# First pair of a GEGLU MLP kernel: the late pieces of x through one PSUM bank, and four products moved ahead of them

## The chip, the cores and the metric

The kernel runs on one core of one Trainium2 chip. The metric is the time of one execution in device microseconds (us). Smaller is better.

PE is the engine of matrix products and transposes, PEld its weight loads, DVE and ACT the two elementwise engines used here, POOL the fourth, SP the engine that issues most DMAs (transfers from the large memory). PE writes into PSUM, a memory of eight banks; the other operands lie in SBUF.

## The reference

```python
# x: 8 x 1024 x 1024, w_gate and w_up: 1024 x 4096, w_down: 4096 x 1024, float32
gate = x @ w_gate
up = x @ w_up
gate = 0.5 * gate * (1 + np.tanh(np.sqrt(2 / np.pi) * (gate + 0.044715 * gate ** 3)))
return ((gate * up) @ w_down).astype(np.float32)
```

## The kernel before

It works in eight passes of 1024 tokens and takes the columns of the two first weights in pairs of 128-column blocks. Nearly all products use a scheme that needs sums of blocks of x and of the weights. The very first pair cannot: its data are still landing. It has its own routine, which casts pieces of x to half precision on DVE, transposes them on PE into a PSUM bank, copies the bank to SBUF, and computes plain products into the eight PSUM banks. K is the dimension that a product sums over; it is taken in two halves (kh). A bank is named by token half (mh), column block (j) and weight (w):

```python
bank = {(mh, j, w): 4 * mh + 2 * j + w ...}          # (1,0,1) is bank 5, (1,1,1) is bank 7

def product(mh, kh, w, j, c=full):                    # 4 matmuls; kh: half of K; c: half or all of the 512 tokens
    for k in range(KH):
        nc.tensor.matmul(ps_all[:, bank[mh, j, w], c], raw(0, 0)[:, w, kh * KH + k, j * P : (j + 1) * P],
                         xq[f"b{kh + 1}{mh + 1}"][:, k, c], start=(kh == 0 and k == 0 and c.start == 0), ...)

def x0_transpose(mh, gp, kh, b, copy):                # 8 transposes into bank b, one copy out of it
    ...
    copy(o, ps)
```

The end of the routine prepares the second pair: a last weight cast, then the four sums of x blocks (`sum_x`, 1.2 us each) and the weight sums (`sum_w`), all on DVE:

```python
    cast_first(0, 1, c1)
    cast_first(1, 1, c1, dve)
    ...                                               # the banks are given back
    sum_x(1); sum_w(0, 1, 0); sum_w(0, 1, 1); sum_x(2)
    outputs(1, 0); outputs(1, 1)
    sum_x(3); sum_w(0, 1, 2); sum_w(0, 1, 3); sum_x(4)
```

## Time and profile before

| what | value |
|---|---|
| time, median of the first 3 runs | 2256.03 us |
| span of the profiled run | 2253.6 us |
| PE busy | 2245.6 us |
| PE waits listed, whole execution | 3.75 us in five places |
| second pair starts on PE (called S) | 27.31 us |
| products on x behind the sums (called M) | 38.16 us |

The timeline of PE in the kernel before (start us, us, engine, line, operation; in brackets the idle time before it and what ended it):

```profile
27.31 3.62 PE L635 MATMUL ps<-x_b,ring 128*128 128x512 f16 x16
30.77 3.73 PE L635 MATMUL ps<-x_sums,ring 128*128 128x512 f16 x16
34.68 3.64 PE L635 MATMUL ps<-x_sums,ring 128*128 128x512 f16 x16 [0.19 <-DVE ring L360]
38.16 3.62 PE L635 MATMUL ps<-x_b,ring 128*128 128x512 f16 x16
```

The second line starts at 30.77 and the third at 34.68, 3.91 us for 16 products that need 3.45. The bracket admits only 0.19, because it counts from the modelled end of the last product (0.38 us each, overlapping; 0.35 between the starts) and because a short stop inside the second group (3.73 against 3.62 us, 0.11) is not broken out.

### The profile page before, as it was taken

The page shows a single profiled execution, that of the slowest core. Times are in us where ns is not written, and L with a number is a line of the kernel's source. Part 1 is how long each engine was busy: PE and PEld are TensorE (multiplying, and loading weights), DVE is VectorE, ACT ScalarE, POOL GpSimd, SP SyncE. Part 2 cuts the span into 40 slices and gives each one's busy share as a digit, 9 for nine tenths or more (in the row PEclk, how much of TensorE's full clock was granted, in tenths as well). Part 3 has the DMA queues.
Part 4 walks back from the last instruction along what each step waited for, and adds up shares of the span by engine and source line. Part 5 has one row for each costly group of instructions (what it writes and reads, how often), then busy time and mean ns, then how long its engine had stood idle before and what let it go on. Part 6 is the DMA issues. An engine that isn't in the chain of part 4 may idle for free.

```text
span 2253.6 us, 42764 instructions
## 1 busy us (share of the span) xinstructions
PE 2245.6 (100%) x16616; PEld 1624.2 (72%) x16616; DVE 1565.1 (69%) x2187; ACT 955.4 (42%) x1863; POOL 674.6 (30%) x825
## 2 busy tenths in 40 slices
PE   9999999999999999999999999999999999999999
PEld 4444444444444445888888888888888888888888
DVE  6666458883588755877776677666786667866674
ACT  4443135651365622666125550356404653055520
POOL 1332013330133300555014540255403543044520
PEclk9999999999999999999999999999999999999999
DMA  9898969999999999999998999988998889998886
GB/s 243 164 210 215 289 180 243 258 270 291 243 229 249 281 304 352 332 343 366 302 337 276 320 309 310 324 267 328 314 322 314 283 310 317 322 309 276 285 292 225
DMA packets 309117, 642.46 MB, mean 285 GB/s; under 512 B 79088, under 2 KB 185328, under 8 KB 288368
## 3 DMA queue, kind: packets, MB, share of 16 engines
q1 hardware_dynamic: 254128, 566.57, 73.5%
q0 software_dynamic: 54784, 73.14, 19.5%
q8 instruction: 130, 2.13, 0.4%
q14 instruction: 75, 0.61, 0.1%
HBM read 574.36 MB, written 138.41 MB: 316 GB/s over the span
## 4 chain that ended last, share of the span: by engine, by line
PE 87%; DMA 2%; SPq 1%; DVE 0%; issue 0%; DVEq 0%
PE ps L857 40%; PE ps L1108 20%; PE ps L635 17%; PE ps L1000 10%; DMA wd_quads<-x_sums 1%; SPq L255 0%; DMA ring<-wd_ops 0%; DVE x_sums L278 0%; DVE h_a L932 0%; DVE tmp L1177 0%; SPq L496 0%; DVEq L278 0%; SPq L544 0%
## 5 line engine op out<-in xcount | busy, mean ns | idle before, releaser
L857 PEld LDWEIGHTS <-ring 128*128 128x128 f16 x8320 | 814.1, 98 | 94.4
L834 POOL TENSOR_TENSOR h_a<-tmp 128x256 f16<-128x256 f32 x640 | 468.0, 750 | 840.6 <-ACT tmp L822 833.5
L857 PE MATMUL ps<-x_sums,ring 128*128 128x256 f16 x5760 | 655.8, 273 | 0.0
L819 DVE TENSOR_TENSOR tmp<-tmp,ps 128x512 f32<-128x512 f32 x640 | 414.3, 683 | 147.1 <-PE ps L857 90.2
L635 PEld LDWEIGHTS <-ring 128*128 128x128 f16 x2632 | 257.4, 98 | 311.2 <-DVE ring L360 0.9
L804 ACT COPY tmp<-ps 128x512 f32<-128x512 f32 x520 | 304.2, 585 | 237.0 <-PE ps L857 163.3
L635 PE MATMUL ps<-x_sums,ring 128*128 128x512 f16 x1504 | 340.1, 379 | 0.2 <-DVE ring L360 0.2
L822 ACT ACTIVATE tmp<-tmp 128x256 f32<-128x256 f32 x640 | 263.7, 418 | 173.2 <-DVE tmp L817 79.5
L857 PE MATMUL ps<-x_b,ring 128*128 128x256 f16 x2560 | 305.6, 273 | 0.0
L817 DVE TENSOR_TENSOR tmp<-ps,tmp 128x512 f32<-128x512 f32 x240 | 165.4, 689 | 145.2 <-ACT tmp L804 99.8
L635 PE MATMUL ps<-x_b,ring 128*128 128x512 f16 x1128 | 259.1, 379 | 0.0
L661 POOL TENSOR_TENSOR h_a<-tmp 128x512 f16<-128x512 f32 x94 | 141.1, 1501 | 377.4 <-ACT tmp L659 265.3
L1108 PEld LDWEIGHTS <-h_a 128*128 128x128 f16 x2240 | 219.2, 98 | 25.3
L1000 PE MATMUL ps<-ring,h_a 128*128 128x512 f16 x1024 | 222.3, 379 | 0.6 <-DMA ring<-wd_ops 0.6
L1108 PE MATMUL ps<-ring,h_a 128*128 128x256 f16 x1920 | 216.1, 273 | 0.0
L1000 PEld LDWEIGHTS <-h_a 128*128 128x128 f16 x1152 | 112.6, 98 | 136.8 <-DMA ring<-wd_ops 1.1
L654 DVE TENSOR_TENSOR tmp<-ps,tmp 128x512 f32<-128x512 f32 x188 | 127.3, 685 | 108.0 <-ACT tmp L646 106.5
L1165 ACT ACTIVATE tmp<-ps 128x512 f32<-128x512 f32 x60 | 35.3, 597 | 362.6 <-PE ps L1108 274.6
L1177 DVE SCALAR_TENSOR_TENSOR tmp<-ps,tmp 128x512 f32<-128x512 f32 x120 | 81.1, 690 | 97.5 <-PE ps L1108 66.7
L360 DVE TENSOR_TENSOR ring<-ring 128x1024 f16<-128x1024 f16 x188 | 139.7, 757 | 11.7 <-DMA ring<-in_w_up_dram 7.5
L646 ACT COPY tmp<-ps 128x512 f32<-128x512 f32 x188 | 109.8, 586 | 77.8 <-PE ps L635 77.8
L1108 PE MATMUL ps<-ring,x_sums 128*128 128x256 f16 x1120 | 126.3, 273 | 0.0
(102 smaller groups left out, 1534.0 us busy)
## 6 DMA issues: line engine op xcount, KB each, us to landing
ring<-w_ops SPq DMA_DIRECT2D x480, 512.0 KB, 4.9
ring<-wd_quads SPq DMA_DIRECT2D x110, 1024.0 KB, 6.9
ring<-wd_ops SPq DMA_DIRECT2D x35, 1024.0 KB, 8.2
out_dram<-tmp SPq DMA_DIRECT2D x128, 256.0 KB, 6.6
w_ops<-h_s SPq DMA_DIRECT2D x128, 256.0 KB, 6.8
ring<-in_w_gate_dram POOLq DMA_DIRECT2D x23, 1024.0 KB, 10.6
ring<-in_w_up_dram POOLq DMA_DIRECT2D x23, 1024.0 KB, 17.9
wd_quads<-x_sums SPq DMA_DIRECT2D x131, 128.0 KB, 6.5
```

The costliest lines, as they stand in the source:

```text
L360: nc.vector.tensor_tensor(o, a, b, op)
L635: nc.tensor.matmul(ps(b, w), lhs[:, k], rhs[:, k, :], start=(first and k == 0), stop=(k == KH - 1), skip_group_check=True,)
L654: nc.vector.tensor_tensor(o, ps("b", w), o, ADD)
L661: nc.gpsimd.tensor_tensor(hq[TO[n]][:, i, :], tmp[:, t[n, 1]], tmp[:, t[n, 0]], MUL)
L804: nc.scalar.copy(tmp[:, t[o[1]]], ps_all[:, bank[o[2]]])
L817: nc.vector.tensor_tensor(d, b, a, SUB)
L819: nc.vector.tensor_tensor(d, a, b, ADD if o[4] == "add" else SUB)
L822: nc.scalar.activation(d, d, GELU, scale=GSC)
L834: nc.gpsimd.tensor_tensor(h, tmp[:, t[o[1]], MQ : 2 * MQ], g, MUL)
L857: nc.tensor.matmul(ps_all[:, bank[c], w * MQ : (w + 1) * MQ], lhs[:, w, k], rhs[:, k], start=(first and w == 0 and k == 0), stop=(k == KH ...
L1000: nc.tensor.matmul(ps_all[:, bank[b, g]], lhs[:, j, g * P : (g + 1) * P], dc[:, n, :], start=(first and j == 0), stop=(j == NP - 1), skip_ ...
L1108: nc.tensor.matmul(ps_all[:, bank[c], m * MQ : (m + 1) * MQ], lhs[:, j, m * P : (m + 1) * P], rhs[:, j, :], start=(first and j == 0 and m ...
```

## The change

The apparent intent: while the second half of x lands, PE should have work. The four products of bank 7 on the first half of K are ready early, but bank 7 was needed for transposes. So the late pieces of x all go through bank 5, bank 7's products move forward, and bank 5's products move to the end.

```diff
         for c in (lo, hi):
             for j in range(2):
                 product(1, 0, 0, j, c)
+        product(1, 0, 1, 1)
         x0_cast(0, 0, 1)
-        x0_transpose(0, 0, 1, 5, act)
         x0_cast(0, 1, 1)
-        x0_transpose(0, 1, 1, 7, dve)
+        x0_transpose(0, 0, 1, 5, dve)
         halves(1)
-        product(1, 0, 1, 0)
+        x0_transpose(0, 1, 1, 5, dve)
         cast_first(1, 1, c0, dve)
         product(0, 1, 0, 0)
         product(0, 1, 0, 1)
         x0_cast(1, 0, 1)
-        x0_transpose(1, 0, 1, 7, act)
+        x0_transpose(1, 0, 1, 5, act)
         x0_cast(1, 1, 1)
         product(0, 1, 1, 0)
         product(0, 1, 1, 1)
-        x0_transpose(1, 1, 1, 7, dve)
+        x0_transpose(1, 1, 1, 5, dve)
...
-            for w, j in ((0, 0), (0, 1), (1, 0)):
+            for w, j in ((0, 0), (0, 1), (1, 1)):
                 product(1, 1, w, j, c)
         for kh in range(2):
-            product(1, kh, 1, 1)
+            product(1, kh, 1, 0)
```

## The prediction

> **What bounds the kernel now.** I read the page first (busy times, then the chain that ended last), then the list of waits of the TensorE (PE), then the timeline of the first 31 us, because the change edits only the routine for the first pair of columns of the first pass.
>
> ```profile
> span 2253.6 us, 42764 instructions
> ...
> PE 2245.6 (100%) x16616; PEld 1624.2 (72%) x16616; DVE 1565.1 (69%) x2187; ACT 955.4 (42%) x1863; POOL 674.6 (30%) x825
> ...
> PE 87%; DMA 2%; SPq 1%; DVE 0%; issue 0%; DVEq 0%
> ```
>
> PE is busy for 2245.6 of 2253.6 us and is 87% of the last chain. Everything else counts only where it makes PE wait. The waits of PE, over the whole execution (total, times, longest):
>
> ```profile
> PE ps L1227 <- DVE h_s L1230: 1.6, 1, 1.6
> PE ps L314 <- DVE h_a L304: 0.7, 1, 0.7
> PE ps L1206 <- ACT x_b L317: 0.7, 1, 0.7
> PE ps L1000 <- DMA ring<-wd_ops: 0.6, 1, 0.6
> PE ps L635 <- DVE ring L360: 0.2, 1, 0.2
> ```
>
> Only the third lies in what is edited. No change of this kind can win more than about 0.7 us, 0.03% of the time. The fourth (at 278.93 us) and the fifth (at 34.68 us) are the two later places where a delay of PE could be taken up again. The timeline around the third (start us, us, engine, line; brackets: idle before, and what ended it):
>
> ```profile
> 14.23 1.98 PE L1206 MATMUL ps<-x_b,ring 128*128 128x256 f16 x16
> 14.44 0.69 DVE L317 COPY x_b<-ps 128x1024 f16<-128x1024 f16 x1 [1.74 <-PE ps L314]
> ...
> 15.04 1.28 DVE L304 TENSOR_SCALAR h_a<-h_a 128x1024 f16<-128x1024 f32 x2
> ...
> 16.05 1.06 PE L314 MATMUL ps<-identity,h_a 128*128 128x128 f16 x16
> ...
> 16.70 1.01 ACT L317 COPY x_b<-ps 128x1024 f16<-128x1024 f16 x1 [2.56 <-PE ps L314]
> ...
> 17.14 0.69 DVE L317 COPY x_b<-ps 128x1024 f16<-128x1024 f16 x1 [0.81 <-PE ps L314]
> ...
> 17.76 2.75 PE L1206 MATMUL ps<-x_b,ring 128*128 128x512 f16 x12 [0.65 <-ACT x_b L317]
> ...
> 19.08 0.69 DVE L304 TENSOR_SCALAR h_a<-h_a 128x1024 f16<-128x1024 f32 x1 [0.65 <-DMA h_a<-in_x_dram]
> 20.34 0.61 PE L314 MATMUL ps<-identity,h_a 128*128 128x128 f16 x8
> 20.44 0.69 DVE L304 TENSOR_SCALAR h_a<-h_a 128x1024 f16<-128x1024 f32 x1 [0.67 <-DMA h_a<-in_x_dram]
> ```
>
> The reader is to see three things. First, the two pieces of x that open the second half of K are cast from 15.04 us on (two casts, no DMA wait in front): they have landed before PE asks for them at 16.05. Second, PE then does both groups of 8 transposes in one go, into banks 5 and 7, and two engines empty the banks side by side (ACT from 16.70, DVE from 17.14). Third, the only gap is that of the next product, which writes bank 5 and therefore waits for ACT's copy to end (16.70 + 1.01 = 17.71, PE starts at 17.76). From there to 27.31 us PE has no wait: the last two pieces of x land at 19.08 and 20.44, and PE takes them only at 20.34 and 22.52.
>
> **What the Trainium skill says.** "PSUM — Partial Sum Buffer", section "PSUM bank collisions raise a hardware error": two engines must not be in one bank and quadrant at once, the hardware doesn't arbitrate, so semaphores must guard by bank. The trace agrees: the wait of 0.65 us ends 0.05 us after the copy out of bank 5. "TensorE: Matmul & The Clock Gate", Part 4 (PE-mode transpose): a transpose lands in PSUM and needs a copy after it, some 275 ns in one kernel, and doesn't count as PE-busy for the clock gate. Here one lasts 219 ns and groups issue at (16.89 - 16.05)/15 = 0.056 us. Same page, Part 1: after at least one idle window of about 3.4 us the array falls to half rate. At the start this trace shows the half rate (weight loads of the first products at 9.29, 9.72, 10.14, 0.43 us apart) and later 0.215 us (12 products in 17.76 to 20.34); it shows no fall back.
>
> **The change part by part.** Bank 7 is product (second half of tokens, w 1, j 1); bank 5 is (same half, w 1, j 0).
>
> 1. *Four matmuls of bank 7 on the first half of K move ahead of the transposes, four of bank 5 move to the end.* PE work is unchanged: 4 x 0.215 = 0.86 us each way. Bank 7 and x are ready (DVE copy ends at 14.44 + 0.69 = 15.13), so they run at 16.05 to 16.91. The old wait of 0.65 us, in issue time 17.76 - (16.05 + 16 x 0.056) = 0.81 us, is gone.
> 2. *Both groups of transposes go through bank 5.* Now transposes, copy, transposes, copy, product are one serial chain with no other PE work inside it. Group one: starts 16.91, last result 0.61 later, 17.52. DVE copies 0.04 later, 17.56, for 0.69, to 18.25. Group two may write bank 5 at 18.30: result 18.91, copy 18.95 to 19.64. The product of the first tokens on the second half of K reads both pieces: 19.70. PE's issue is empty from 16.91 + 0.45 = 17.36 to 18.30 (0.94) and from 18.75 to 19.70 (0.95): 1.89 us.
> 3. *Net on PE.* Before, that product began four matmuls after 17.76, at 18.62. After: 19.70. That is +1.08 us, equal to 1.89 - 0.81.
> 4. *Copy by DVE in place of ACT (0.69 for 1.01).* It shortens the first link by 0.32, already in the sum. DVE then does its weight cast at 19.65 to 20.33 and the next x cast to 21.0; PE asks for that piece at 19.70 + 8 x 0.215 = 21.42. No wait.
> 5. *The last two pieces also through bank 5.* Transposes at 21.42, ACT copy to about 23.04; 8 matmuls stand between, to 23.58, so bank 5 is free when the last group comes. DVE copy to about 24.95; the half-width products between (12 x 0.11 = 1.3, from 24.03) hide it. No wait.
> 6. *To the end of the pair.* From there 4.35 us of products as before (22.96 to 27.31): next pair at 28.38 instead of 27.31, +1.07.
> 7. *Behind it.* DVE's chain of sums starts at 27.40, after a wait of 2.27 us for a weight piece, so DMA and not PE sets it; its outputs end at some 26.4 instead of 25.1, still in time. So the sums come when they came, and the wait of 0.19 us at 34.68 vanishes. Left: about +0.9 us. At 278.93 PE waits 0.60 us for a load of wd_ops. The chain in front of it goes through small stores and DVE sums; DVE follows PE there without a gap from about 204 to 232 us (its step at 209.30 was released by PE), and the queue's loads wait for PE. So that wait moves with PE and takes up little. From 278.93 on PE runs without a wait: the delay reaches the end.
>
> Sum: 1.08 - 0.19 = +0.89, to which I add 0.1 for the chance of a clock fall (below): 2256.03 + 1.0 = **2257.0 us**.
>
> **The rivals.**
> *The fill pays.* If x landed late, four matmuls ready to run would be worth up to the old gap, 0.81: about 2255.2. Against it: no DMA wait stands before the casts at 15.04, so PE was not waiting for x but for the copies; the fill is spent before the gap opens. I give it 7%.
> *The delay is taken up later.* If the load at 278.93 keeps its own time, 0.60 goes: +0.3, about 2256.3. For: a chain of DMAs stands before it, and their landing varies. Against: the DVE and queue waits in front of it follow PE. 20%.
> *The clock falls.* Between 16.91 and 19.70 only transposes run: 2.79 us (before: 17.76 - 16.05 = 1.71). By the page's window of 3.4 us this is too short; if a partly idle window were enough, one window at half rate costs some 1.7 us, two 3.4: about 2259 to 2260. 8%.
> *DVE becomes the bound.* One more copy, 0.69 us, against an idle stretch of 2.27 before 27.40. It would need another 1 us of lateness; the waits at 30 to 37 us would then grow. 5%, some +1.5.
>
> **Range and chances.** The main path gives 2256.9, repeats of the kernel before spread over 0.6 us, and the take-up at 278.93 can move it by as much. The pull of the late clock case makes the upper side longer: 2255.7 to 2258.3. All cases lie inside 0.2% of the time before, so within 2% is near certain: faster 0.01, same 0.98, slower 0.01.
>
> **What would show each step right or wrong.** In the timeline of after: 4 full products directly behind the half-width ones at about 16.05; two separate groups of 8 transposes at 16.9 and 18.3 with two DVE copies between; two waits of PE on DVE's x_b copies, about 0.75 to 0.95 us each, in place of the one on ACT; the first product of the second half at 19.7; the next pair at 28.4; no PE wait near 34.7; matmuls still 0.215 us apart. Wrong would be: PE going on with other work during the copies, x landing after 16 us in that run, the next pair starting before 27.3, or the wait near 279 us shrinking by as much as PE is late.

## More of the kernel before

The granted clock is the share of its full rate that PE was given, 1.000 at most.

S and M are read from the timeline of PE. Between them lie 48 products of 512 columns, first 16 on x and then 32 on sums of x; they issue 0.2155 us apart, so M - S is 10.34 us if PE never stops. Here it is 10.85: PE stands still for about half a microsecond in all.

## The result and the profile after

| | median | range | runs |
|---|---|---|---|
| before, same rounds and the first three | 2255.91 us | 2254.71 to 2256.97 | 6 |
| after | 2255.53 us | 2255.22 to 2257.07 | 6 |

The ratio is 0.9999, with a 95% interval of 0.9986 to 1.0012: no difference that these runs could show. A ratio here is the mean time of one kernel's fast runs over the mean of the other's fast runs of the same rounds, so it is not quite the ratio of the medians above. The predicted 2257.0 was too high, and the measured median lies 0.17 us below the range.

Yet the trace after shows the local loss almost as it was worked out. The list of PE's waits in the changed kernel (total us, times, longest):

```profile
PE ps L1227 <- DVE h_s L1230: 1.6, 1, 1.6
PE ps L314 <- DVE x_b L317: 0.8, 1, 0.8
PE ps L1206 <- DVE x_b L317: 0.8, 1, 0.8
PE ps L314 <- DVE h_a L304: 0.8, 1, 0.8
PE ps L1000 <- DMA ring<-wd_ops: 0.4, 1, 0.4
```

The single wait on ACT's copy (0.7) has become two waits on DVE's copies (0.8 each), and the wait on DVE's weight sums (0.2) is gone. The timeline of the changed kernel around them:

```profile
14.15 2.84 PE L1206 MATMUL ps<-x_b,ring 128*128 128x256 f16 x20
...
16.83 0.61 PE L314 MATMUL ps<-identity,h_a 128*128 128x128 f16 x8
17.48 0.69 DVE L317 COPY x_b<-ps 128x1024 f16<-128x1024 f16 x1 [1.23 <-PE ps L314]
18.22 0.61 PE L314 MATMUL ps<-identity,h_a 128*128 128x128 f16 x8 [0.78 <-DVE x_b L317]
...
18.86 0.69 DVE L317 COPY x_b<-ps 128x1024 f16<-128x1024 f16 x1 [0.70 <-PE ps L314]
...
19.61 1.89 PE L1206 MATMUL ps<-x_b,ring 128*128 128x512 f16 x8 [0.78 <-DVE x_b L317]
...
28.30 3.62 PE L635 MATMUL ps<-x_b,ring 128*128 128x512 f16 x16
...
31.75 7.07 PE L635 MATMUL ps<-x_sums,ring 128*128 128x512 f16 x32
...
38.66 3.62 PE L635 MATMUL ps<-x_b,ring 128*128 128x512 f16 x16
```

Transposes, copy, transposes, copy, product now stand one behind the other. From the start of the half-width products to the first product on the second half of K it takes 19.61 - 14.15 = 5.46 us; before it took 18.62 - 14.23 = 4.39. That is the +1.07 of the prediction. The second pair starts 0.99 later (28.30 against 27.31). But M comes only 0.50 later (38.66 against 38.16): behind S, PE now runs 48 products without a stop. In this pair of traces, half of the loss has been given back within 10 us.

### The profile page after: what moved, and what is told of

Same layout as the page of the kernel before. It is cut to its first block, busy times and chain, and to the rows that moved or that the text cites. A ratio compares the mean times of both kernels' runs of the same rounds, so it can differ in the third digit from the quotient of the medians.

```text
span 2254.2 us, 42763 instructions
## 1 busy us (share of the span) xinstructions
PE 2245.5 (100%) x16616; PEld 1624.4 (72%) x16616; DVE 1563.9 (69%) x2188; ACT 955.6 (42%) x1862; POOL 684.5 (30%) x825
## 4 chain that ended last, share of the span: by engine, by line
PE 84%; DMA 3%; DVE 1%; SPq 1%; issue 0%; ACT 0%; POOL 0%; POOLq 0%; DVEq 0%
PE ps L857 40%; PE ps L1108 20%; PE ps L635 14%; PE ps L1000 10%; DMA ring<-in_w_up_dram 2%; DMA wd_quads<-x_sums 1%; SPq L255 0%; DMA ring<-wd_ops 0%; DVE ring L360 0%; DVE x_sums L278 0%; DVE h_a L672 0%; DVE h_s L278 0%; DVE tmp L654 0%; POOL ring L345 0%; DVE h_a L932 0%
## 5 line engine op out<-in xcount | busy, mean ns | idle before, releaser
L661 POOL TENSOR_TENSOR h_a<-tmp 128x512 f16<-128x512 f32 x94 | 149.7, 1592 | 367.8 <-ACT tmp L659 265.4
```

What stands on the lines that cost most here:

```text
L661: nc.gpsimd.tensor_tensor(hq[TO[n]][:, i, :], tmp[:, t[n, 1]], tmp[:, t[n, 0]], MUL)
```

## The experiments

All outputs are right. "Same call" means the runs of the kernel before on the same chip in the same rounds (9 each). S and M as above; the last trace column is when PE begins the products behind a load of wd_ops (prepared blocks of the third weight), with the wait listed there. From M to that point PE needs 240.0 us without a stop. In filled_sums PE's wait is listed under a step of DVE; its weight load waited 1.85 us for the load there, as in the others.

| run | S | M | M - S | behind the load (wait) | mean less mean of before, same call |
|---|---|---|---|---|---|
| before | 27.31 | 38.16 | 10.85 | 278.93 (0.60) | |
| null_before | 27.05 | 38.21 | 11.16 | 278.60 (0.23) | -0.41 |
| after | 28.30 | 38.66 | 10.36 | 279.25 (0.42) | -0.15 (6 runs of each) |
| after_again | 27.64 | 38.15 | 10.51 | 279.11 (0.79) | +0.49 |
| after_third | 27.68 | 38.18 | 10.50 | 278.19 (none) | +0.19 |
| before_sums | 26.96 | 37.37 | 10.41 | 279.31 (1.06) | -0.41 |
| after_sums | 27.51 | 37.87 | 10.36 | 278.82 (0.78) | -0.25 |
| delay_5 | 28.42 | 38.78 | 10.36 | 278.79 (none) | +0.38 |
| delay_20 | 31.07 | 41.43 | 10.36 | 281.44 (none) | +4.04 |
| filled | 27.25 | 38.26 | 11.01 | 278.99 (0.56) | +0.25 |
| filled_sums | 27.27 | 37.63 | 10.36 | 279.16 (1.36) | -0.36 |
| filled_sums_2 | 27.30 | 37.66 | 10.36 | 278.14 (0.31) | -0.77 |
| fill_between | 27.10 | 38.12 | 11.02 | 278.43 (none) | -0.21 |

My theory after the result was *take-up*: PE's lateness of up to half a microsecond costs nothing, because the sums on DVE hold PE between S and M anyway. The rivals: it is only noise; the load near 279 takes the lateness up; or the change costs nothing at all.

### How large the noise is, and the mean of the changed kernel

Two unchanged kernels, the second one twice.

> The kernel before, unchanged, timed against itself: it measures the noise. If the miss of the prediction is noise of the runs (the noise theory), single runs spread over 2 us or more and the ratio of the means differs from 1 by some 0.0001 to 0.0003 although nothing differs. If repeats agree within 0.3 us, the noise theory falls and the time of the changed kernel is really no longer than before. Trace: second pair starts on PE at 27.3 us, the products on x_b that follow the sums at 38.2, the first product behind the wait near 279 at 278.9 plus or minus 0.5.

> The changed kernel, unchanged. Take-up theory: of the 1.0 us that PE is late at the start of the second pair (28.3), only 0.5 is left at the products on x_b after the sums (38.7 against 38.2), and 0.3 to 0.5 at 500 us and at the end, so the mean is 0.3 to 0.5 us over that of the null run. My prediction as written: 0.9 left at both marks and at the end. Third view (no cost at all): as fast as the null run within 0.1 us.

> The changed kernel a third time, for the mean: so far 11 runs of it average 2255.89 and 29 of the kernel before 2255.44. Take-up theory: again 0.3 to 0.6 over the kernel before of the same call. Third view (no cost): the difference is 0.0 or negative again, as in the first result. Prediction as written: 1.0.

The kernel before, run against itself, came out 0.41 us faster than itself (2255.10 against 2255.51, ratio 0.9998). Its own five runs were close (2254.66 to 2255.38), but the nine beside it went from 2254.68 to 2256.27. So differences of 0.4 between five and nine runs mean nothing by themselves. Put together, 47 runs of the kernel before over all calls average 2255.41 (2254.37 to 2256.97; standard deviation 0.61, standard error 0.09), and 16 runs of the changed kernel average 2255.78 (2254.68 to 2257.49; standard error 0.20). The difference is +0.37 us, give or take some 0.4. Within the three calls of the changed kernel it is -0.15, +0.49 and +0.19, weighted by runs +0.16, with about the same doubt. Either fits the take-up theory, neither fits the 1.0 I had added, and no cost at all is not excluded by time alone.

The three calls also show that S itself moves: 28.30, 27.64 and 27.68 for the same changed kernel. It is not the edited part that moves it: from the start of the half-width products to S it takes 14.15 us in all three (28.30 - 14.15, 27.64 - 13.49, 27.68 - 13.54), and 13.08 in before and null_before, so the local loss is 1.07 whatever the start. What differs lies in front: the first 12 products took 3.35 us from 9.29 in before, and 2.75 from 9.19 in after_third. M moves less, 38.66, 38.15 and 38.18. So in two of the three traces nothing of the loss is left at M; the three average 38.33, against 38.19 in before and null_before. Where S lies below about 27.8 and the sums are not moved, M sits at 38.12 to 38.26 (before, null_before, after_again, after_third, filled, fill_between), which is what a limit set by another engine looks like. The trace of null_before, where PE came to the sums early, names it (DVE's sums of x, then its sums of weights):

```profile
31.80 2.75 PE L635 MATMUL ps<-x_sums,ring 128*128 128x512 f16 x12 [0.27 <-DVE x_sums L267]
34.74 3.64 PE L635 MATMUL ps<-x_sums,ring 128*128 128x512 f16 x16 [0.18 <-DVE ring L360]
```

### The sums on DVE moved forward

The same edit in both kernels: the first two sums of x go into DVE's idle stretch before the last weight cast.

```diff
+        sum_x(1)
+        sum_x(2)
         cast_first(0, 1, c1)
         cast_first(1, 1, c1, dve)
...
-        sum_x(1)
         sum_w(0, 1, 0)
         sum_w(0, 1, 1)
-        sum_x(2)
```

> The kernel before with the first two sums of x (1.2 us each on DVE) put in front of DVE's cast of the last weight piece, into its idle stretch of 2.3 us. Take-up theory: PE is held by this chain of sums near 31.7 and 34.7 us; with the sums earlier both gaps (0.46 in issue time) go: second pair still at 27.3, products on x_b at 37.7 instead of 38.2, the end 0.4 earlier. Rival (the gap at 34.7 is only the 0.19 of the list of waits): 38.0 and 0.2 earlier.

> The changed kernel with the same two sums moved forward. Take-up theory: PE never waited for the sums in the changed kernel, so nothing is gained: second pair at 28.3, products on x_b at 38.7 as in the changed kernel, and against the kernel before with sums moved the full 1.0 us now stays. Rival (the take-up has nothing to do with the sums): the difference of the two kernels at that mark stays 0.5, that is 38.2 here.

The timeline of PE in the kernel before with the sums moved:

```profile
26.96 3.67 PE L635 MATMUL ps<-x_b,ring 128*128 128x512 f16 x16
30.46 7.07 PE L635 MATMUL ps<-x_sums,ring 128*128 128x512 f16 x32
37.37 3.62 PE L635 MATMUL ps<-x_b,ring 128*128 128x512 f16 x16
41.18 1.02 PE L635 MATMUL ps<-x_sums,ring 128*128 128x512 f16 x4 [0.20 <-DVE h_a L672]
```

The two groups on sums are now one unbroken run of 32, as in the changed kernel: M - S falls from 10.85 to 10.41. In the changed kernel the same edit leaves M - S at the 10.36 of its first trace (10.51 and 10.50 in the two others, where S came earlier). This shows the take-up: the stop between S and M was the wait for the sums, and PE's lateness in the changed kernel had only filled it. The marks themselves were not those expected, because S came early in both runs: S is 0.55 apart and M 0.50 (37.87 against 37.37), where I had said 1.0; what decides is that none of the 0.55 is lost between S and M. The rest of the expectation failed in part too: in before_sums PE, now early, met new stops on DVE at 41.18 and 42.38. They are listed as 0.20 and 0.18, but between the starts they are 0.36 and 0.34, so that at the next mark (46.71 against 46.79) only 0.08 of the lead of 0.79 was left. Then came a wait of 1.06 at the load near 279. The mean was 0.41 under its call, and after_sums lay 0.15 over before_sums (standard error some 0.6); neither can be told from nothing.

### A delay without the change

Dummy products behind the last product of the first pair, in the kernel before; here 5 of them, and 20 in the second run.

```diff
+        warm(5)
         cast_first(0, 1, c1)
```

> The kernel before with 5 dummy matmuls of 0.215 us behind the first pair's last product (1.08 us in PE's queue): the size of the delay that the change makes, without the change. Take-up theory: second pair at 28.4, products on x_b at 38.7 (0.5 of the 1.08 is taken up), end 0.3 to 0.6 later. Prediction as written: 39.0 and 0.9 later.

> The same with 20 dummy matmuls, 4.31 us. Take-up theory: a fixed 0.5 is taken up at the sums (products on x_b at 42.0, 3.8 late) and at most some 0.2 more near 279, so the end is 3.6 to 3.8 later. Rival (the load near 279 keeps its own time): at most 0.6 more is taken up there, 3.2 later. Rival (delays in the first pair never reach the end): under 1 later.

```profile
19.68 0.62 PE L314 MATMUL ps<-identity,h_a 128*128 128x128 f16 x8 [0.35 <-DVE h_a L304]
...
22.54 0.62 PE L314 MATMUL ps<-identity,h_a 128*128 128x128 f16 x8 [0.51 <-DVE h_a L304]
...
28.42 3.62 PE L635 MATMUL ps<-x_b,ring 128*128 128x512 f16 x16
31.87 7.07 PE L635 MATMUL ps<-x_sums,ring 128*128 128x512 f16 x32
38.78 3.62 PE L635 MATMUL ps<-x_b,ring 128*128 128x512 f16 x16
```

With the delay alone (delay_5, 1.08 us) S and M are those of the changed kernel's first trace to about a tenth: 28.42 and 38.78, M - S 10.36. In part that is chance: here PE began the half-width products early, at 13.05, and lost the lead again in front of the last two groups of transposes, where it waited for casts of x (the first two lines). With the delay of 4.31 us M - S is 10.36 too: what the sums take up is a fixed half microsecond, not a share. (M came at 41.43, not at the 42.0 that I expected, because the first pair ended at 26.75 in that execution.) In time it cost 4.04 in the mean of its call, with a standard error of some 0.5: the idea that delays in the first pair never reach the end falls, but 3.8, 4.3 and even the 3.2 of the other rival cannot be told apart. The profiled run of delay_20 was its fastest (2257.87; the others 2258.87 to 2260.24). In it PE was 3.27 us later than in the trace of before at M and 2.51 later behind the load.

What the load near 279 does stays open. Its wait went from none to 1.36 us: none in after_third, whose PE came at 278.2, and 0.79 in after_again, whose PE came at the same time. A delay of about 3 us mostly passes it: in delay_20, act_first_2 and act_both (the last two below) PE was 3.0 us late at M in the mean and 2.7 behind the load (281.44, 280.82 and 282.40; in act_both it waited there again), so the load does come later when PE is much later. For less than a microsecond, which is the question here, the traces look otherwise. Three with M at 37.6 to 37.9 came out of it at 278.71 in the mean, seven with M at 38.1 to 38.3, and before_sums, at 278.89, and three with M at 38.4 to 38.8 at 278.84 (act_first and act_first_fill included): 0.1 apart where M is 0.9 apart, as if the load kept its own time. Single traces scatter as much (278.14 to 279.54), and against it stand the run times of filled_sums_2 below, 0.77 under its call where less than 0.2 was expected if the load kept its own time. Behind the load there is one more place of this kind: in after_third and act_first PE waited for DVE and ACT between 414 and 446 us, and from the load to the end took 1975.6 us, where all other traces took 1974.6 to 1975.2.

### Work inside the chain of bank 5

First the smallest edit of the changed kernel, one line moved:

```diff
-        product(1, 0, 1, 1)
         x0_cast(0, 0, 1)
         x0_cast(0, 1, 1)
         x0_transpose(0, 0, 1, 5, dve)
         halves(1)
+        product(1, 0, 1, 1)
         x0_transpose(0, 1, 1, 5, dve)
```

> The changed kernel with one step moved: the four products of bank 7 stand between the two groups of transposes instead of in front of both. Chain theory: they then cover the first copy out of bank 5, only one wait on a copy (0.78) is left instead of two, and from the start of the half-width products to the first product on the second half of K it takes 4.5 to 4.7 us (changed kernel 5.46, before 4.39). Rival (the fill must come first, while x lands): no shorter than 5.4. Behind the sums 10.9 to 11.2 after the start of the second pair, PE waiting for DVE again.

The stretch took 17.73 - 13.14 = 4.59 us instead of 5.46, one wait of 0.78 on a copy was left, and M - S grew to 11.02. All as the chain theory says: the four products were worth 0.87 us, but behind the first transposes, not in front of them. They do not need to run while x lands; they need to run while a copy does. The mean was 0.21 under its call, not to be told from nothing. S gained less: from the half-width products to it this run took 27.10 - 13.14 = 13.96 us, where 13.08 + 0.20 was to be expected, because PE, early here, stood again in front of the last two groups of transposes (0.20 listed on a cast of x at 22.30).

Then the full version: in addition half-width products on the first piece while the second is copied, the last but one group of transposes one product further on (the last stays where it was, other than the expectation says), and all copies by DVE; without and with the sums moved forward.

```diff
         cast_first(1, 1, c0, dve)
-        product(0, 1, 0, 0)
-        product(0, 1, 0, 1)
+        for c in (lo, hi):
+            for j in range(2):
+                product(0, 1, 0, j, c)
         x0_cast(1, 0, 1)
-        x0_transpose(1, 0, 1, 5, act)
-        x0_cast(1, 1, 1)
         product(0, 1, 1, 0)
+        x0_transpose(1, 0, 1, 5, dve)
+        x0_cast(1, 1, 1)
         product(0, 1, 1, 1)
```

> The changed kernel with PE work put inside the serial chain of bank 5: the four products of bank 7 between the two groups of transposes, half-width products on the first piece while the second is copied, and the last two groups moved one product on. If the chain transposes, copy, transposes, copy is what costs the 1.9 us of gaps, the gaps fall to under 0.3 and the second pair starts at 26.6 to 26.9, 0.5 before the kernel before. Take-up theory: PE is then held by the sums on DVE instead, products on x_b at 38.1 to 38.2, so the end gains nothing against the kernel before. Rival (PE's lead passes): 37.6 and 0.5 earlier.

> The same with the two sums moved forward. Take-up theory: both limits are gone, second pair at 26.6 to 26.9, products on x_b at 37.1 to 37.3, the end 0.8 to 1.0 us before the kernel before (ratio 0.9996). If the sums are not the limit, it equals the run without them moved.

> The version with both limits lifted, a second time, to see whether its lead of 0.4 us in the means (2254.86 against 2255.23) holds: take-up theory 0.3 to 0.6 under the kernel before. If the wait near 279 keeps its own time (it stood between 278.6 and 279.3 in eight traces whatever the lateness of PE), the lead is under 0.2.

```profile
22.44 0.62 PE L314 MATMUL ps<-identity,h_a 128*128 128x128 f16 x8 [0.83 <-DVE h_a L304]
...
34.79 3.64 PE L635 MATMUL ps<-x_sums,ring 128*128 128x512 f16 x16 [0.19 <-DVE ring L360]
```

These lines are PE's only two listed waits in filled between 6 and 270 us. The waits on the copies are gone, but S is 27.25, not the 26.6 to 26.9 I expected: PE now stands before the last transposes, because the last piece of x is cast only at 21.69 (at 20.44 in the trace of before). The landing of x limits PE when it comes early, and not in this order alone: in delay_5 and fill_between it waited for casts of x too. From there 0.46 us of transposes and 4.35 of products lead to S. And the little lead that was left ended at the sums (M 38.26), as expected. With the sums moved too, S was again 27.27 and 27.30, and M came 0.6 earlier (37.63 and 37.66), not at the expected 37.1 to 37.3. Ten runs of that version average 2254.72 (2254.06 to 2255.62), 0.36 and 0.77 under the kernel before of their calls. It has the lowest mean, about 0.7 us under the 47 runs, or 0.03%: visible in the means, and of no use in practice.

### How long PE may go without products

One copy handed back to ACT, to see whether each link of the chain counts:

```diff
-        x0_transpose(0, 0, 1, 5, dve)
+        x0_transpose(0, 0, 1, 5, act)
```

> The changed kernel with one part undone: the first copy out of bank 5 by ACT (1.01 us) again instead of DVE (0.69). Chain theory: in a serial chain every link counts, so the same stretch takes 5.46 + 0.32 = 5.78 us and the first wait of PE grows from 0.78 to 1.10. Rival (which engine copies does not matter, as in the kernel before, where two copies ran side by side): 5.46.

In the trace the stretch took 19.41 - 13.56 = 5.85 us (expected 5.78), and PE's first wait was 1.10. But the mean was 1.82 us over its call, and four of the five runs had a granted clock of 0.999, the other 1.000. No other kernel had shown that. So the rival to which the prediction gave 8% came back, and three more runs followed: both copies by ACT; the first by ACT but the four products between the transposes; and the same kernel again.

```diff
 # act_both, against act_first
-        x0_transpose(0, 1, 1, 5, dve)
+        x0_transpose(0, 1, 1, 5, act)
 # act_first_fill, against fill_between
-        x0_transpose(0, 0, 1, 5, dve)
+        x0_transpose(0, 0, 1, 5, act)
```

> The changed kernel with both copies out of bank 5 by ACT, which makes the stretch in which PE does only transposes longer still: 2.8 us in the changed kernel, 3.4 with the first copy by ACT, here about 4.1 (the two weight casts of ACT stand between the copies). Clock theory: this stretch sets PE back to a slower clock, so the granted clock is 0.999 or 0.998 in most runs, a trace shows products more than 0.3 us apart after the stretch, and the time is 2258 or more. Rival (plain lateness): clock 1.000, 1.3 us later than the changed kernel at the start of the second pair, time some 2257.0.

> First copy by ACT as in the slow run, but the four products of bank 7 between the two groups of transposes, so that no stretch without products is longer than about 1.9 us. Clock theory: clock 1.000 in all runs and time within 0.5 us of the kernel before. Rival (the copy by ACT itself, or this chip on that day, costs the 1.8 us): clock 0.999 and about 2257 again.

> The slow run of the last call again. Clock theory: again some runs with the granted clock at 0.999 and over 2256.5, others at 1.000 and near 2256.0; if the profiled one is of the first kind, products behind the stretch are 0.43 us apart instead of 0.215 for a while. Rival (chance of that call): clock 1.000 throughout and a mean near 2256.1 (0.3 over the changed kernel).

This time the profiled run was one of the slow ones. PE in act_first_2, then its engines by stretch of 2 us (busy time of each engine; the third column from the end is the granted clock):

```profile
18.63 0.61 PE L314 MATMUL ps<-identity,h_a 128*128 128x128 f16 x8 [1.10 <-ACT x_b L317]
20.09 2.96 PE L1206 MATMUL ps<-x_b,ring 128*128 128x512 f16 x8 [0.86 <-DVE x_b L317]
22.85 1.06 PE L314 MATMUL ps<-identity,h_a 128*128 128x128 f16 x8
```

```profile
18.00:20.00 2.00, 0.61 (x8) 0.52 (x8) 0.65 (x2) 1.61 (x3) 0.00 (x0) 1.00 1.08 384
20.00:22.00 2.00, 1.91 (x7) 0.72 (x7) 1.84 (x4) 0.00 (x0) 0.00 (x0) 0.69 1.06 345
22.00:24.00 2.00, 2.00 (x12) 1.31 (x11) 0.00 (x0) 0.05 (x1) 0.00 (x0) 0.50 1.10 348
24.00:26.00 2.00, 2.00 (x15) 1.04 (x14) 0.00 (x0) 2.00 (x4) 0.97 (x2) 0.96 0.77 243
```

Some 0.7 us behind the end of the second wait the clock falls to half (0.69 over the stretch from 20 to 22 means from about 20.76 on) and it comes back at about 24.16, after 3.4 us: what is missing in the last three rows is 2 x (0.31 + 0.50 + 0.04) = 1.7 us. The trace of act_both shows such a fall too, behind 20.72. From the start of the half-width products to S this run took 30.46 - 14.24 = 16.22 us and the run of act_first with the clock at 1.000 took 28.10 - 13.56 = 14.54: 1.68 lost, as the prediction had estimated for one window (1.7). The length of the stretch in which PE does transposes alone, from the timelines, and the clock:

| kernel | transposes alone | runs at clock 0.999 | mean less before, same call |
|---|---|---|---|
| before | 17.76 - 16.05 = 1.71 us | 0 of 41 with a clock on record | |
| act_first_fill | 18.77 - 16.91 = 1.86 | 0 of 5 | +0.60 |
| after | 19.61 - 16.83 = 2.78 | 0 of 16 | +0.37 (all runs) |
| act_first, act_first_2 | 19.41 - 16.24 = 3.17 | 8 of 10 | +1.82, +1.19 |
| act_both | 20.72 - 17.05 = 3.67 | 5 of 5 | +3.43 |

(The stretches were a little shorter than the 3.4 and 4.1 that I had written beforehand, and act_first_fill was 0.60 over its call where I had said 0.5 at most.) With the same copy by ACT but the stretch cut in two, the clock stays: it is the stretch, not the copy. The edge lies somewhere between 2.78 and 3.17 us, so the changed kernel stays below it by 0.4 us at most. Whether its slowest runs (2257.07 and 2257.49) met it in part is open. Their clock reads 1.000; a loss of 1.7 us in 2254 would lower it to 0.999, but a half clock of up to some 2 us (1 us lost) would not show, and no profile of such a run exists. Nor does the record show all: at the start of before it reads 1.00, while weight loads of products are 0.43 us apart (9.29, 9.72, 10.14).

## Why the prediction was right or wrong

**Steps 1 to 6: right.** Two waits on DVE's copies for one on ACT's, transposes at 16.83 and 18.22 (predicted 16.91 and 18.30), the first product of the second half at 19.61 (19.70), the second pair at 28.30 (28.38), the local cost 1.07 (1.08). The later transposes through bank 5 made no wait, though with less to spare than step 5 thought: the last piece of x was cast at 21.74 after a DMA wait of 0.98, not at 20.44. The rival that the fill pays was rightly given little: in the trace of before PE had not been waiting for x.

**Step 7, first half: the step that failed, by size.** It said that "the wait of 0.19 us at 34.68 vanishes. Left: about +0.9 us". The mechanism is the right one, DVE's sums do hold their time. But the term was 0.49, not 0.19: 0.99 late at S, 0.50 at M, in the first pair of traces; in the two other traces of the changed kernel nothing was left at M. The run before_sums and the two delays show that it is the sums. I had read the old wait on ACT in issue time (0.81 for a listed 0.65) and this one from the list, which gave 0.19 for the 0.35 between starts and left out a stop of 0.11. M - S, 10.85 against 48 x 0.2155, would have told it from the profile of before.

**Step 7, second half: not shown.** It said that the load near 279 moves with PE and takes up little, so that "the delay reaches the end". A delay of 3 us mostly did. For one below a microsecond the traces leave open whether the load takes up a part or all of it, which is the rival that the prediction gave 20%. Its wait scatters from none to 1.36 us, more than the 0.6 that the range allowed for it.

**The base: off by 0.6.** The prediction added its cost to 2256.03, the median of three runs, and took their spread of 0.6 us for the noise. 47 runs average 2255.41 and spread over 2.6. With both terms put right, 2255.41 + 1.07 - 0.49 = 2255.99; the mean of 16 runs is 2255.78 with a standard error of 0.20. What remains is of the size of the noise: the median of the first six runs, 2255.53, lies 0.26 under their own mean. The third part of the miss is the 0.1 added for a fall of the clock, of which no run of this kernel gave a sign. Here the prediction had some luck: it held its 2.79 us against a window of 3.4, and 3.17 was enough for a fall in 8 of 10 runs.

## What to carry to other kernels

Filling work helped here only where it stood inside the wait: look up what PE waits for, here a copy out of a bank and not the landing of data, and put the fill behind the instruction that starts that copy. Read a stop from the distance of the starts of two groups, not from a listed idle time, and ask which engine's next fixed time will swallow a gain or a loss before adding it to the end. Before predicting a change of a microsecond, get the mean and the spread of the base from more than three runs.

## What the Trainium skill lacked or had wrong

- "TensorE: Matmul & The Clock Gate", Part 1, gives an idle window of about 3.4 us for the fall to half clock and says that it is free-running. The runs agree with the half clock (0.50 in the trace of act_first_2, for some 3.4 us) but put the edge lower for a stretch that holds transposes: 2.78 us showed no fall in 16 runs, 3.17 us did in 8 of 10, 3.67 us in 5 of 5. The same page, section "Why this matters for your kernels", warns of idle gaps over about 3 us, and that fits the runs better.
- "PSUM — Partial Sum Buffer" tells why a bank must be guarded, but no page says what a whole turn of one bank costs: transposes, copy and the two hand-overs took 18.22 - 16.83 = 1.39 us here, of which PE stood idle for all but 0.45.
